# Two linked edits in an fp32 encoder trunk: block products accumulated over several blocks in the same PSUM banks, and the mixer's normalized input made on VectorE

## The chip, the cores and the metric

The kernel runs on one core of a Trainium2 chip. The metric is device time in microseconds of one execution. The kernel before takes 2313.22 us, the median of three runs that lie between 2312.47 and 2314.23.

In a profile, PE is TensorE, PEld its loading of weights, DVE VectorE, ACT ScalarE, POOL GpSimd, and SP the engine whose queue issues the transfers from and to memory.

## The reference

The program is a trunk of two layers over 512 positions and 1,024 features, in float32. Each layer is a half-step feed-forward network (FFN), a mixer, a second FFN and a gated embedding:

```python
for i in range(DEPTH):                                     # DEPTH = 2
    h = h + 0.5 * swiglu(rmsnorm(h, ffn1_norm[i]), ffn1_w_gu[i], ffn1_w_down[i])
    hn = rmsnorm(h, mix_norm[i])
    h = h + (ssd_mixer(hn, ...) if i % 2 == 0 else neighbourhood_attention(hn, ...))
    h = h + 0.5 * swiglu(rmsnorm(h, ffn2_norm[i]), ffn2_w_gu[i], ffn2_w_down[i])
    gate = jax.nn.sigmoid(rmsnorm(h, ple_norm[i]) @ ple_w_gate[i])
    h = h + gate * rmsnorm(p[i] @ ple_w_proj[i], ple_post_norm[i])

def swiglu(x, w_gu, w_down):                               # w_gu [1024, 5632], w_down [2816, 1024]
    g, u = jnp.split(x @ w_gu, 2, axis=-1)
    return (jax.nn.silu(g) * u) @ w_down
```

The mixer of layer 0 is a bidirectional state-space scan (SSD), which begins with a projection of `hn` to 8,256 columns; that of layer 1 is a neighbourhood attention.

## The kernel before

**Layout.** Features lie on the 128 partitions, positions on the free axis. h is 8 tiles of 128 x 512, and a weight is used in tiles of 128 x 128. TensorE accumulates in PSUM, in banks of 128 x 512 float32. Eight banks are in use: five of the kind `mm` and three of the kind `px`.

**Products in two halves.** Each operand is split into a high half, which is the value rounded to the fp32r type, and a low half, the rest. A product is then three: weight-high by x-high, weight-high by x-low, weight-low by x-high. `gemm` (lines 278, 281, 282) issues these three for 512 columns. The halves of a weight come from `split_raw`: a cast on ACT (L221) and a subtraction on DVE (L223). They are made by `prep_next` up to three units ahead of their use. Loads are issued on SP's queue (`load_unit`, `top_up`), and the order of units, which sets the order of loads too, is written out by `plan`. x is split by `split` (L303 to L307).

**FFN.** An FFN has 22 tiles of its inner width. The first few (`gate_up`, six in the first FFN, four in the others) are plain products. The others go in pairs of tiles, and each pair is computed by a scheme of seven products of half size in place of eight: x is cut into two halves of features and two halves of 256 positions, `sums` makes sums and differences of these (one set for each of kk = 0 to 3), `prep_next` makes sums and differences of the four weight matrices (L243, L246, L254), and `block(p, i)` with i = 0 to 6 multiplies the two. One block is 24 products of 256 columns: 2 output tiles, 4 tiles of features, and the three products of L508, L509 and L510. The four FFNs have 35 pairs, so 245 blocks. `block` takes a bank for each block and adds the results up from there (L514 on DVE, L518 on ACT), with `halve` splitting what goes into the second multiplication. Between blocks stand the products with the down weights, of 512 columns, eight per chunk of 14 or 21 blocks. `ffn_order` sets the sequence.

**SSD's start.** From h and the factor R of the norm (a row of 512, on all partitions) the normalized input is made: POOL multiplies by R (L687), and `split` then applies the gain in its cast on ACT (L306) and in its subtraction on DVE (L307). The steps of the scan's time constant (`steps`), the convolution (L748, L756) and the projection share the engines with this.

**What sets the order.** Each engine works through its own queue in order; a scheduler fixes the queues when the program is built, from the order in which the code is written and its estimate of durations, and puts in the waits. Buffers come from pools with a fixed number of slots; a new tile waits for the last reader of the slot's old one.

## Time and profile before

| | |
|---|---|
| time, median of 3 runs | 2313.22 us (2312.47 to 2314.23) |
| the profiled execution's own time | 2312.72 us |
| its span, first to last instruction | 2310.9 us |
| granted clock of TensorE, mean | 0.999 |
| DVE, POOL instructions | 2613, 269 |
| moved by DMA | 281.69 MB |

The page gives each engine's busy time and its share of the span, then the span in 40 slices, then the chain of work that ended last, then groups of instructions by line, operation and operands. A row of a group has the count, the busy time in us, the mean ns of one, and after the second bar the idle time of the engine just ahead of them with what ended it. A row of a timeline has the start, the duration, the engine, the line, the output and the inputs, the shape and the count; in square brackets it has the idle time before and what ended it. A row of waits has the us in total, how often, and the longest. A row of windows has the length and, by engine, the busy us with the count, then the granted clock, the share of the DMA engines and GB/s. Durations of neighbours on an engine can overlap, so the distance between two starts is the price of the first.

### The profile page before, as it was taken

Reading aid. Unit: us, or ns where it says so; the run is one execution under the profiler, and the core shown is the slowest. Engines: PE = TensorE matmul, PEld = TensorE weight load, DVE = VectorE, ACT = ScalarE, POOL = GpSimd, SP = SyncE. Lnnn points to the kernel's source line nnn. Section 1 sums busy time; section 2 is a strip of 40 time slices with the busy share of each in tenths; the row PEclk is TensorE's granted clock in tenths of the full one; section 3 lists DMA queues with packets and bytes.
Section 4 is the critical chain, followed back from the end, with each engine's and each line's share of the span. In section 5 each row is a group of like instructions: output and inputs, shape, how many; then the busy total and the mean of one; then the engine's idle time right before and its main releaser. Section 6 shows DMA issues by size and latency. Waiting matters only on the chain.

```text
span 2310.9 us, 35433 instructions
## 1 busy us (share of the span) xinstructions
PE 2294.1 (99%) x13732; PEld 2027.0 (88%) x13732; DVE 1828.3 (79%) x2613; ACT 1179.8 (51%) x2038; POOL 339.1 (15%) x269
## 2 busy tenths in 40 slices
PE   9999999999999999999999999999999999999999
PEld 8899997888888888999998889999878888999987
DVE  8878868878888958987875897887578859888866
ACT  5433445776767864443445443444446755444452
POOL 0000003255554651000003100000110010000020
PEclk9999999999999999999999999999999999999999
DMA  5323323444444643332223222232557732333222
GB/s 189 118 77 109 105 85 108 160 160 138 145 145 138 189 171 118 102 101 94 90 90 109 102 101 96 93 106 78 169 183 208 228 116 87 110 105 101 87 92 73
DMA packets 105224, 281.69 MB, mean 122 GB/s; under 512 B 13136, under 2 KB 14032, under 8 KB 105056
## 3 DMA queue, kind: packets, MB, share of 16 engines
q1 hardware_dynamic: 104768, 279.30, 37.3%
q8 instruction: 107, 1.75, 0.3%
q14 instruction: 61, 0.50, 0.1%
q10 hardware_dynamic: 288, 0.14, 0.0%
HBM read 259.70 MB, written 13.40 MB: 118 GB/s over the span
## 4 chain that ended last, share of the span: by engine, by line
PE 94%; DVE 3%; ACT 1%; DMA 1%; POOL 1%; issue 0%; SPq 0%; ACTq 0%
PE ps L278 19%; PE ps L281 19%; PE ps L282 19%; PE ps L510 10%; PE ps L509 10%; PE ps L508 10%; PE ps L930 1%; PE ps L889 1%; DVE wl L223 1%; PE ps L910 1%; PE ps L1325 1%; PE ps L1271 1%; DVE t L756 1%; PE ps L834 1%; POOL t L687 1%; PE ps L845 1%
## 5 line engine op out<-in xcount | busy, mean ns | idle before, releaser
L278 PE MATMUL ps<-md,wh 128*128 128x512 f32 (+1 forms) x2032 | 799.4, 394 | 2.6 <-ACT wh L221 1.8
L282 PE MATMUL ps<-md,wl 128*128 128x512 f32 (+1 forms) x2032 | 791.5, 390 | 2.8 <-DVE wl L223 2.8
L281 PE MATMUL ps<-md,wh 128*128 128x512 f32 (+1 forms) x2032 | 792.2, 390 | 0.0
L221 ACT CAST wh<-wr 128x1024 fp32r<-128x1024 f32 (+2 forms) x395 | 351.8, 892 | 491.7 <-PE ps L281 249.8
L223 DVE TENSOR_TENSOR wl<-wr,wh 128x1024 fp32r<-128x1024 f32 (+2 forms) x395 | 418.9, 1062 | 86.4 <-ACT wh L221 84.5
L282 PEld LDWEIGHTS ps<-md,wl 128*128 128x128 f32 x2032 | 382.1, 188 | 85.3 <-DVE wl L223 4.9
L278 PEld LDWEIGHTS ps<-md,wh 128*128 128x128 f32 x2032 | 382.8, 188 | 76.6 <-ACT wh L221 2.3
L281 PEld LDWEIGHTS ps<-md,wh 128*128 128x128 f32 x2032 | 382.8, 188 | 71.6
L221 ACT CAST wh<-md 128x1024 fp32r<-128x1024 f32 x175 | 183.6, 1049 | 322.6 <-PE ps L509 293.7
L332 POOL TENSOR_TENSOR sq<-sq,sq 128x512 f32<-128x512 f32 x71 | 101.0, 1423 | 1636.9 <-ACT sq L328 1632.5
L510 PE MATMUL ps<-sc,wl 128*128 128x256 f32 x980 | 277.6, 283 | 0.8 <-DVE wl L223 0.8
L508 PE MATMUL ps<-sc,wh 128*128 128x256 f32 x980 | 277.0, 283 | 0.8 <-ACT wh L221 0.8
L509 PE MATMUL ps<-md,wh 128*128 128x256 f32 x980 | 277.6, 283 | 0.1
L510 PE MATMUL ps<-md,wl 128*128 128x256 f32 x980 | 277.4, 283 | 0.0
L509 PE MATMUL ps<-sc,wh 128*128 128x256 f32 x980 | 277.3, 283 | 0.0
L508 PE MATMUL ps<-md,wh 128*128 128x256 f32 x980 | 277.2, 283 | 0.0
L514 DVE TENSOR_TENSOR t<-ps,t 128x512 f32<-128x512 f32 x245 | 165.9, 689 | 137.3 <-PE ps L510 136.6
L223 DVE TENSOR_TENSOR wl<-md,wh 128x1024 fp32r<-128x1024 f32 x175 | 213.6, 1220 | 16.1 <-ACT wh L221 15.7
L508 PEld LDWEIGHTS ps<-sc,wh 128*128 128x128 f32 x980 | 187.7, 192 | 4.9 <-ACT wh L221 1.0
L509 PEld LDWEIGHTS ps<-sc,wh 128*128 128x128 f32 x980 | 187.8, 192 | 3.8
L509 PEld LDWEIGHTS ps<-md,wh 128*128 128x128 f32 x980 | 188.1, 192 | 1.6 <-DVE md L472 0.4
L508 PEld LDWEIGHTS ps<-md,wh 128*128 128x128 f32 x980 | 188.1, 192 | 1.3
(209 smaller groups left out, 2913.2 us busy)
## 6 DMA issues: line engine op xcount, KB each, us to landing
wr<-in_w_gw_dram SPq DMA_DIRECT2D x70, 512.0 KB, 3.6
md<-in_w_gw_dram SPq DMA_DIRECT2D x70, 512.0 KB, 5.1
wr<-in_w_in_dram SPq DMA_DIRECT2D x65, 512.0 KB, 3.5
wr<-in_w_dn_dram SPq DMA_DIRECT2D x128, 256.0 KB, 2.7
wr<-in_w_gu_dram SPq DMA_DIRECT2D x32, 512.0 KB, 3.5
hs<-crow SPq DMA_DIRECT2D x64, 256.0 KB, 3.6
wr<-in_w_dn_dram SPq DMA_DIRECT2D x32, 384.0 KB, 3.1
wr<-in_w_qkv_dram SPq DMA_DIRECT2D x24, 512.0 KB, 4.3
```

The source lines that it names most:

```text
L221: splits.append(s.copy(out=hi[:, :n], in_=raw[:, :n]))
L223: v.tensor_sub(out=lo[:, :n], in0=raw[:, :n], in1=hi[:, :n])
L278: m = te.matmul(out=pt, lhsT=hi[:, sl], rhs=part(xp, 0, cols), start=first and k == 0, stop=False)
L281: te.matmul(out=pt, lhsT=hi[:, sl], rhs=part(xp, 1, cols), start=False, stop=False)
L282: gemm.last = te.matmul(out=pt, lhsT=lo[:, sl], rhs=part(xp, 0, cols), start=False, stop=last and k == n - 1)
L332: (v if fast else g).tensor_add(out=self.acc, in0=self.acc, in1=q)
L508: te.matmul(out=o, lhsT=hi[:, sl], rhs=xh, start=j == 0 and kk == 0, stop=False)
L509: te.matmul(out=o, lhsT=hi[:, sl], rhs=xl, start=False, stop=False)
L510: te.matmul(out=o, lhsT=lo[:, sl], rhs=xh, start=False, stop=j == 1 and kk == 3)
L514: v.tensor_add(out=k[to], in0=pt, in1=k[other])
L687: g.tensor_mul(out=t, in0=hk[k], in1=R)
L756: v.scalar_tensor_tensor(out=a[:, lo:hi], in0=src[:, lo + o:hi + o], scalar=w(j), in1=a[:, lo:hi], op0=ALU.mult, op1=ALU.add)
```

## The change

Blocks 0, 1, 2 and 6 no longer have a bank each. They accumulate in the same two banks (one for each output tile), one after the other, each starting from what the last one left. x's high and low half for them lie side by side in one tile of 512, so weight-high multiplies both as one product of 512 columns, and weight-low the high half as one of 256: 16 products per block instead of 24. A bank then holds the product with x's low half in its upper 256 columns and the rest in its lower 256; `whole` reads both parts and adds them, by a copy on ACT and an addition on DVE for each half. Blocks 3 and 5 accumulate in one bank in the old form, and block 4 has one. The order of blocks becomes 0, 3, 1, 5, 2, 4, 6, and the preparation of the next pair's weights stands at the same positions of the sequence as before. `sums` casts and subtracts in half pieces of 256. At SSD's start, POOL's multiplication and the gain are one operation on DVE, followed by a plain cast on ACT and a plain subtraction on DVE. The first product `cbm` of the first group takes a bank of the other kind.

```diff
--- before.py
+++ after.py
@@ -47,6 +47,9 @@
+TURN = (0, 3, 1, 5, 2, 4, 6)
 def ffn_order(chunks):
@@ -55,7 +58,7 @@
         a, b = chunks[c]
-        blocks = [(p, i) for p in range(a // 2, b // 2) for i in range(7)]
+        blocks = [(p, i) for p in range(a // 2, b // 2) for i in TURN]
         d = 0
...
@@ -166,8 +169,8 @@
                         yield "o", a
-                        if a[1] >= 4 and a[0] < NF // 2 - 1:
-                            yield from ahead(a[0] + 1, a[1] - 4)
+                        if a[1] in TURN[4:] and a[0] < NF // 2 - 1:
+                            yield from ahead(a[0] + 1, TURN.index(a[1]) - 4)
                     elif what == "down":
...
@@ -449,7 +452,7 @@
         xs = [[None] * 4 for _ in range(7)]
-        x11 = []
+        spare = []
...
@@ -461,15 +464,12 @@
                                        op1=ALU.mult)
-            if kk == 0:
-                x11[:] = [sc_r(), sc_r()]
-            elif kk == 2:
+            if kk == 2:
                 m = md(F32R)
-                x11[:] = m[:, 0, :], m[:, 1, :]
-            c = slice(HT * (kk % 2), HT * (kk % 2) + HT)
-            hl = x11[0][:, c], x11[1][:, c]
-            s.copy(out=hl[0], in_=x[0][:, lo_])
-            v.tensor_sub(out=hl[1], in0=x[0][:, lo_], in1=hl[0])
+                spare[:] = m[:, 0, :], m[:, 1, :]
+            hl = spare.pop(0) if spare else sc_r()
+            s.copy(out=hl[:, lo_], in_=x[0][:, lo_])
+            v.tensor_sub(out=hl[:, hi_], in0=x[0][:, lo_], in1=hl[:, lo_])
             xs[0][kk] = hl
...
@@ -481,68 +481,77 @@
                 return m[:, 0, :], m[:, 1, :]
-            (ah, al), (bh, bl) = room(), room()
             a, b = t2(), t2()
...
             v.tensor_sub(out=b[:, hi_], in0=x[1][:, lo_], in1=a[:, hi_])
-            for x_, hh, ll in ((a, ah, al), (b, bh, bl)):
-                s.copy(out=hh, in_=x_)
-                v.tensor_sub(out=ll, in0=x_, in1=hh)
-            for i, hh, ll, c in ((3, ah, al, lo_), (1, ah, al, hi_), (2, bh, bl, lo_), (6, bh, bl, hi_)):
-                xs[i][kk] = hh[:, c], ll[:, c]
+            for x_, two in ((a, (3, 1)), (b, (2, 6))):
+                for i, c, hl in zip(two, (lo_, hi_), room()):
+                    s.copy(out=hl[:, lo_], in_=x_[:, c])
+                    v.tensor_sub(out=hl[:, hi_], in0=x_[:, c], in1=hl[:, lo_])
+                    xs[i][kk] = (hl[:, lo_], hl[:, hi_]) if i == 3 else hl
...
-            pt = mm_bank()
+            k = kept
             hi, lo = unit()
+            chain = {0: "a", 1: "a", 2: "a", 6: "a", 3: "b", 5: "b", 4: "c"}[i]
+            opens, wide_ = i in (0, 3, 4), chain == "a"
+            if opens:
+                k[chain] = [mm_bank() for _ in range(1 + wide_)]
+            pt = k[chain]
+            mm = lambda o, w, x, st, sp_: te.matmul(out=o, lhsT=w, rhs=x, start=opens and st, stop=sp_,
+                                                    skip_group_check=not opens)
             for j in range(2):
...
                     sl = slice((4 * j + kk) * P, (4 * j + kk + 1) * P)
-                    o = pt[:, j * HT:(j + 1) * HT]
-                    xh, xl = xs[i][kk]
-                    te.matmul(out=o, lhsT=hi[:, sl], rhs=xh, start=j == 0 and kk == 0, stop=False)
-                    te.matmul(out=o, lhsT=hi[:, sl], rhs=xl, start=False, stop=False)
-                    te.matmul(out=o, lhsT=lo[:, sl], rhs=xh, start=False, stop=j == 1 and kk == 3)
-            k = kept
-            def add(to, other):
-                v.tensor_add(out=k[to], in0=pt, in1=k[other])
-            if i == 0:
-                k["s"] = t2()
-                s.copy(out=k["s"], in_=pt)
-            elif i == 1:
-                k["u"] = t2()
-                add("u", "s")
+                    last = kk == 3 and (wide_ or j == 1)
+                    if wide_:
+                        both = xs[i][kk]
+                        mm(pt[j], hi[:, sl], both, kk == 0, False)
+                        mm(pt[j][:, :HT], lo[:, sl], both[:, :HT], False, last)
+                    else:
+                        o = pt[0][:, j * HT:(j + 1) * HT]
+                        xh, xl = xs[i][kk]
+                        mm(o, hi[:, sl], xh, j == 0 and kk == 0, False)
+                        mm(o, hi[:, sl], xl, False, False)
+                        mm(o, lo[:, sl], xh, False, last)
+            def whole(to, more=False):
+                for j in range(2):
+                    o = to[:, j * HT:(j + 1) * HT]
+                    if more:
+                        v.tensor_add(out=o, in0=pt[j][:, HT:], in1=o)
+                    else:
+                        s.copy(out=o, in_=pt[j][:, HT:])
+                    v.tensor_add(out=o, in0=pt[j][:, :HT], in1=o)
+            if i in (0, 1):
+                to = "su"[i]
+                k[to] = t2()
+                whole(k[to])
+            elif i == 3:
+                k["q"] = t2()
+                s.copy(out=k["q"], in_=pt[0])
+            elif i in (5, 4):
+                to = "u" if i == 5 else "s"
+                v.tensor_add(out=k[to], in0=pt[0], in1=k[to])
+                s.activation(out=k[to], in_=k[to], func=AF.Silu)
             elif i == 2:
-                k["v"] = t2()
-                add("v", "u")
-            elif i == 3:
-                k["w"] = t2()
-                add("w", "v")
-                add("u", "u")
-            elif i == 4:
-                add("s", "s")
-                s.activation(out=k["s"], in_=k["s"], func=AF.Silu)
+                whole(k["q"], True)
+                v.tensor_mul(out=k["q"], in0=k["q"], in1=k["u"])
+                k["hl"] = md(F32R), md(F32R)
+                for j in range(2):
+                    mids[2 * p + j] = tuple(y[:, j, :] for y in k["hl"])
+                halve(k["hl"], k["q"], slice(HT, T))
             else:
-                if i == 5:
-                    add("u", "u")
-                    s.activation(out=k["u"], in_=k["u"], func=AF.Silu)
-                    x, gate, c = k["w"], k["u"], slice(HT, T)
-                    k["hl"] = md(F32R), md(F32R)
-                    for j in range(2):
-                        mids[2 * p + j] = tuple(y[:, j, :] for y in k["hl"])
-                else:
-                    add("v", "v")
-                    x, gate, c = k["v"], k["s"], slice(0, HT)
-                v.tensor_mul(out=x, in0=x, in1=gate)
-                halve(k["hl"], x, c)
+                w = t2()
+                whole(w)
+                v.tensor_mul(out=k["s"], in0=w, in1=k["s"])
+                halve(k["hl"], k["s"], slice(0, HT))
...
@@ -684,9 +693,9 @@
             t = t2()
-            g.tensor_mul(out=t, in0=hk[k], in1=R)
+            v.scalar_tensor_tensor(out=t, in0=hk[k], scalar=col(norm.gain + k), in1=R, op0=ALU.mult, op1=ALU.mult)
             xn.append(md(F32R))
-            split(xn[k], t, col(norm.gain + k))
+            split(xn[k], t, None)
...
@@ -840,7 +849,7 @@
             for dr in range(2):
-                pt = (mm_bank, px_bank)[dr]()
+                pt = (mm_bank if gi and dr == 0 else px_bank)()
                 for c in range(NC):
...
```

Line numbers shift: L223 becomes L226, L254 L257, L278, L281 and L282 become L281, L284 and L285, the products of a block are all L506, the split of the combinations of x (L492 and L493) is L491 and L492, the drains are L527, L529 and L530.

**The first place: TensorE, where the blocks of the third FFN begin.** Before, from the end of the first block (`wl_13108` is its weight's low half) into the second (`wl_13157`):

```order
L508 MATMUL ps_13193<-md_13084,wh_13106 128x256
L509 MATMUL ps_13193<-md_13084,wh_13106 128x256
L510 MATMUL ps_13193<-md_13084,wl_13108 128x256
L510 MATMUL ps_13230<-sc_12933,wl_13157 128x256
L508 MATMUL ps_13230<-sc_12995,wh_13155 128x256
L509 MATMUL ps_13230<-sc_12996,wh_13155 128x256
L510 MATMUL ps_13230<-sc_12995,wl_13157 128x256
L508 MATMUL ps_13230<-sc_13090,wh_13155 128x256
```

Now, from the end of block 0 (`wl_12744`) into block 3 (`wl_12797`):

```order
L506 MATMUL ps_12842<-md_12716,wh_12742 128x512
L506 MATMUL ps_12842<-md_12716,wl_12744 128x256
L506 MATMUL ps_12843<-md_12716,wl_12744 128x256
L506 MATMUL ps_12843<-md_12716,wh_12742 128x512
L506 MATMUL ps_12843<-md_12716,wl_12744 128x256
L506 MATMUL ps_12870<-sc_12562,wh_12795 128x256 x2
L281 MATMUL ps_12897<-md_12543,wh_12832 128x512
L284 MATMUL ps_12897<-md_12543,wh_12832 128x512
L506 MATMUL ps_12870<-sc_12562,wl_12797 128x256
L506 MATMUL ps_12870<-sc_12629,wh_12795 128x256 x2
L506 MATMUL ps_12870<-sc_12629,wl_12797 128x256
```

Block 0 alternates between products of 512 columns, with x's two halves in one operand, and of 256, and fills two banks. Two down products (L281, L284) have moved ahead of the next block's first product with its low half.

**The second place: VectorE at the same stretch.** L490 and L493 make combinations of x and their low halves, `wl_13157` is the weight's low half as above, L440 is the next plain product's. Before:

```order
L304 TENSOR_TENSOR md_13140<-t_13136,md_13140 128x512
L489 TENSOR_TENSOR t_13145<-t_13136,t_13145 128x256
L223 TENSOR_TENSOR wl_13157<-md_12871,wh_13155 128x1024
L490 TENSOR_TENSOR t_13146<-t_13136,t_13145 128x256
L493 TENSOR_TENSOR md_13143<-t_13145,md_13143 128x512
L254 TENSOR_TENSOR md_12871<-md_12789,md_12871 128x1024
L493 TENSOR_TENSOR md_13144<-t_13146,md_13144 128x512
L440 TENSOR_TENSOR t_13184<-ps_13104,rt_12899 128x512
L443 TENSOR_TENSOR t_13187<-ps_13105,rt_12899 128x512
```

Now, with `wl_12797` the weight's low half that TensorE's second block reads:

```order
L307 TENSOR_TENSOR md_12776<-t_12772,md_12776 128x512
L487 TENSOR_TENSOR t_12779<-t_12772,t_12779 128x256
L492 TENSOR_TENSOR md_12785<-t_12779,md_12785 128x256
L488 TENSOR_TENSOR t_12780<-t_12772,t_12779 128x256
L492 TENSOR_TENSOR md_12790<-t_12780,md_12790 128x256
L492 TENSOR_TENSOR md_12785<-t_12779,md_12785 128x256
L492 TENSOR_TENSOR md_12790<-t_12780,md_12790 128x256
L226 TENSOR_TENSOR wl_12797<-md_12493,wh_12795 128x1024
L443 TENSOR_TENSOR t_12823<-ps_12740,rt_12523 128x512
```

Four half pieces (L492) and L488 stand ahead of the weight's low half. Before, L490 and both L493 stood behind it, and so did L254, which is further back now.

**The third place: VectorE at SSD's start.** L681 scales the time constant, L748 the first product of the convolution, and `wl_3725` is the low half of the projection's weight that follows, and L756 is the convolution. Before, from the sixth of eight residuals (L307):

```order
L307 SCALAR_TENSOR_TENSOR md_3693<-t_3691,cst,md_3693 128x512
L307 SCALAR_TENSOR_TENSOR md_3698<-t_3696,cst,md_3698 128x512
L307 SCALAR_TENSOR_TENSOR md_3703<-t_3701,cst,md_3703 128x512
L748 TENSOR_TENSOR t_3711<-ps_3621,rt_3648 128x512
L223 TENSOR_TENSOR wl_3725<-wr_3569,wh_3723 128x1024
L756 SCALAR_TENSOR_TENSOR t_3713<-t_3711,ccw,t_3713 128x510
L223 TENSOR_TENSOR wl_3767<-wr_3575,wh_3765 128x1024
```

Now the same stretch's end, from the fifth of eight multiplications (L696) to the weight's low half `wl_3549`:

```order
L696 SCALAR_TENSOR_TENSOR t_3510<-hs_82,cst,rt_3472 128x512
L696 SCALAR_TENSOR_TENSOR t_3515<-hs_83,cst,rt_3472 128x512
L696 SCALAR_TENSOR_TENSOR t_3520<-hs_84,cst,rt_3472 128x512
L307 TENSOR_TENSOR md_3512<-t_3510,md_3512 128x512
L696 SCALAR_TENSOR_TENSOR t_3525<-hs_85,cst,rt_3472 128x512
L307 TENSOR_TENSOR md_3517<-t_3515,md_3517 128x512
L307 TENSOR_TENSOR md_3522<-t_3520,md_3522 128x512
L307 TENSOR_TENSOR md_3527<-t_3525,md_3527 128x512
L757 TENSOR_TENSOR t_3535<-ps_3445,rt_3472 128x512
L226 TENSOR_TENSOR wl_3549<-wr_3393,wh_3547 128x1024
```

Ahead of these stand L690 (which was L681), four L696 and four L307. DVE has 16 pieces where it had eight; POOL's queue is eight rows shorter.

## The prediction, made before the changed kernel ran

> **What bounds the kernel now.** I read the page first: shares, slices, the chain that ended last, the groups.
>
> ```profile
> span 2310.9 us, 35433 instructions
> PE 2294.1 (99%) x13732; PEld 2027.0 (88%) x13732; DVE 1828.3 (79%) x2613; ACT 1179.8 (51%) x2038; POOL 339.1 (15%) x269
> PEclk9999999999999999999999999999999999999999
> PE 94%; DVE 3%; ACT 1%; DMA 1%; POOL 1%; issue 0%; SPq 0%; ACTq 0%
> ...
> L510 PE MATMUL ps<-sc,wl 128*128 128x256 f32 x980 | 277.6, 283 | 0.8 <-DVE wl L223 0.8
> L514 DVE TENSOR_TENSOR t<-ps,t 128x512 f32<-128x512 f32 x245 | 165.9, 689 | 137.3 <-PE ps L510 136.6
> ```
>
> PE is busy for 99% of the span at full granted clock in all 40 slices, and the chain runs 94% through it. So the time is the sum of PE's steps, plus the few places where PE waits. Two things can move it: what a product costs PE, and whether PE waits more or less. The six 256-column groups (L508 to L510, 980 each) are the 5,880 products of 245 blocks. Their 283 ns of busy time overlaps the next product, so I take pace from starts on PE's timeline, in the SSD's projection and in the second FFN.
>
> ```profile
> 388.28 0.39 PE L281 MATMUL ps<-md,wh 128*128 128x512 f32 x1
> ...
> 401.88 0.39 PE L281 MATMUL ps<-md,wh 128*128 128x512 f32 x1
> ...
> 1001.58 0.39 PE L282 MATMUL ps<-md,wl 128*128 128x512 f32 x1
> 1001.81 0.28 PE L508 MATMUL ps<-sc,wh 128*128 128x256 f32 x1
> 1001.92 0.28 PE L509 MATMUL ps<-sc,wh 128*128 128x256 f32 x1
> ...
> 1004.56 0.28 PE L510 MATMUL ps<-md,wl 128*128 128x256 f32 x1
> 1004.68 0.40 PE L278 MATMUL ps<-md,wh 128*128 128x512 f32 x1
> 1004.91 0.40 PE L281 MATMUL ps<-md,wh 128*128 128x512 f32 x1
> 1005.15 0.39 PE L282 MATMUL ps<-md,wl 128*128 128x512 f32 x1
> ```
>
> The first two rows are 60 starts apart: 13.60/60 = 0.2267 us for 512 columns. From 1001.92 to 1004.56 lie 22 starts: 0.120 us for 256. Two narrow products cost 0.240, one wide 0.2267; the 13.3 ns between them is a cost per product, whatever its width.
>
> **Part 1, wide products.** Blocks 0, 1, 2 and 6 of each of 35 pairs (140 blocks) form eight groups of one 512- and one 256-column product instead of three of 256: 140 × 8 = 1,120 products fewer. Each group goes from 0.360 to 0.2267 + 0.120 = 0.3467 us, so the gain is 1,120 × 13.3 ns = **14.9 us**. What no row shows is the strict alternation of widths. The nearest rows are the switches above: 0.11 to 0.12 for a narrow product, 0.23 for a wide one beside it, 0.34 to 0.35 together (gain 11 to 22 us). The 0.24 at 1004.91 bounds it from the other side: with it the group costs 0.36 and the gain is nothing. I take the even paces, which lie inside the switches' range.
>
> The page "TensorE: Matmul & The Clock Gate" of the Trainium skill (section "Wait — 56ns, not 53.3ns?") puts the fixed cost of a warm matmul at about 2.5 ns; by it this term would be an estimated 2.8 us and the time 2308. The rows above show 13.3 ns between two narrow and one wide product, and the rows decide.
>
> **Part 2, chains and their drains.** Banks now accumulate over several blocks, and the next block of a chain can't start before the last value is read. Per pair DVE's seven full adds become two full and ten half ones, and ACT gets six half copies more. Rows that price them, from DVE's timeline at the second FFN's start, the groups by shape and the page's DMA issues:
>
> ```profile
> 944.83 0.68 DVE L304 TENSOR_TENSOR md<-t,md 128x512 fp32r<-128x512 f32 x1
> 945.43 0.42 DVE L489 TENSOR_TENSOR t<-t,t 128x256 f32<-128x256 f32 x1
> 945.77 1.22 DVE L223 TENSOR_TENSOR wl<-md,wh 128x1024 fp32r<-128x1024 f32 x1
> 946.90 0.42 DVE L490 TENSOR_TENSOR t<-t,t 128x256 f32<-128x256 f32 x1
> ...
> L698 ACT COPY sc<-ps 128x256 f32<-128x256 f32 x1 | 0.4, 353 | 0.0
> ...
> wr<-in_w_gw_dram SPq DMA_DIRECT2D x70, 512.0 KB, 3.6
> ```
>
> Steps (start to start) are 0.34 for a half piece, 0.60 for a full one and 1.13 for 1,024 columns. DVE gets 10 × 0.34 + 2 × 0.60 − 7 × 0.60 = 0.4 us more per pair, ACT 6 × 0.35 = 2.1. Over a steady stretch of blocks, and where the second FFN begins:
>
> ```profile
> core 0: us, PE busy (x) PEld busy (x) DVE busy (x) ACT busy (x) POOL busy (x), PEclk, DMA share, GB/s
> 915.00:955.00 40.00, 40.00 (x207) 34.30 (x206) 40.00 (x68) 24.11 (x36) 0.00 (x0) 1.00 0.27 87
> 990.00:1247.00 257.00, 257.00 (x1730) 238.32 (x1729) 198.23 (x248) 114.60 (x152) 13.84 (x10) 1.00 0.30 96
> ```
>
> In blocks DVE is busy for 198 of 257 us and ACT for 115; with the additions about 81% and 52%, so they fit beside PE. The order 0, 3, 1, 5, 2, 4, 6 puts another block (2.88 us, 24 × 0.12) and mostly a down product between two links. At the tightest place, the last chunk, where block 3 alone lies between 0 and 1, block 1 may start 8 × 0.3467 + 2.88 = 5.65 us after block 0 began. DVE's work queued there (0.60, 1.13, 0.60, 1.13 and two adds of 0.34, and 0.08 for the last one's tail) is done at 4.2. That leaves 1.4 us; a steady pair, walked in the same way, leaves 1.9. I cost the hand-overs at **0**; the cover is block 3, and without it each would cost up to those 2.9 us less the slack.
>
> On SP's queue one weight load moves ahead of a down load, and block 2's matrix is held two positions longer, so the load that takes its place starts later. It lands after 3.6 us; DVE has four pieces of 1.13 (4.5 us) to do before it reads that matrix. So again 0, with about 1 us of room; without it the loss would be under 1 us per pair and lie with the rival of slow hand-overs.
>
> **Part 3, FFN starts.** Here x's combinations are made while the first blocks begin, and DVE has no gap: 40.00 of 40.00 above. Each of four sets now takes four half subtractions instead of two full ones (+0.14 each). Worse, DVE's order puts four half pieces ahead of the low half of the second block's weight, where L490 and one of the full pieces came after it. The third FFN shows what that meets.
>
> ```profile
> PE ps L508 <- ACT wh L221: 0.8, 1, 0.8
> PE ps L510 <- DVE wl L223: 0.8, 1, 0.8
> ...
> 1354.64 1.21 DVE L223 TENSOR_TENSOR wl<-md,wh 128x1024 fp32r<-128x1024 f32 x1
> 1355.78 0.41 DVE L490 TENSOR_TENSOR t<-t,t 128x256 f32<-128x256 f32 x1
> ...
> 945.15 0.28 PE L508 MATMUL ps<-sc,wh 128*128 128x256 f32 x1
> ```
>
> The low half comes 0.34 (L490) + 4 × 0.34 + 3 × 0.14 = 2.1 us later. In the third FFN PE waits for it already, so all of **2.1** is lost. In the second, block 0 began at 945.15, the low half was wanted 26 products later (948.27) and was there at 946.90. Now it is there at 949.0 and wanted at 948.6 (block 0 is shorter by 0.11, two wide down products go ahead of it): 0.4 lost, and some 0.6 with the next low half: **1.0**. The fourth has the second's order, **1.0**; the first has room, **0.2**. Sum **+4.3 us**, ends 0 (the pieces fit) and 13 (each start trips the slow clock below and loses 1.6 to 2 us more).
>
> **Part 4, SSD's start.** POOL's eight multiplications go to DVE. Waits of PE between 340 and 450 us, and the timelines and clock around them:
>
> ```profile
> PE ps L282 <- DVE wl L223: 2.3, 2, 1.5
> PE ps L278 <- ACT wh L221: 1.8, 1, 1.8
> PE ps L716 <- DVE md L712: 1.4, 1, 1.4
> PE ps L278 <- DVE sc L848: 0.8, 1, 0.8
> ...
> 382.48 0.50 PE L278 MATMUL ps<-md,wh 128*128 128x512 f32 x1 [1.83 <-ACT wh L221]
> 384.06 0.50 PE L282 MATMUL ps<-md,wl 128*128 128x512 f32 x1 [0.85 <-DVE wl L223]
> ...
> 384.60:388.00 3.40, 3.40 (x9) 0.50 0.65 220
> ...
> 367.96 0.68 DVE L681 TENSOR_TENSOR t<-ps,rt 64x512 f32<-64x512 f32 x1 [1.87 <-ACT rt L359]
> 368.01 12.73 POOL L687 TENSOR_TENSOR t<-hs,rt 128x512 f32<-128x512 f32 x8 [10.75 <-ACT rt L359]
> 381.52 0.75 DVE L307 SCALAR_TENSOR_TENSOR md<-t,cst,md 128x512 fp32r<-128x512 f32 x1 [0.24 <-ACT md L306]
> 381.40 1.98 ACT L221 CAST wh<-wr 128x1024 fp32r<-128x1024 f32 x2
> ```
>
> POOL needs 12.7 us; ACT's casts and DVE's subtractions follow it one by one, and the weight's cast stands behind the last, at 381.40. Now DVE does 0.60 (L681) + 8 × 0.66 (the 0.75 of 381.52 less the 0.08 by which its rows overlap) + 8 × 0.60 from 367.96, is through at 378.6, and after L748's successor (0.60) and the subtraction (1.22) the low half is there at 380.5. PE wanted it at 382.48 − 1.83 + 2 × 0.2267 = 381.1. So the 1.83 and the 0.85 go, and with them the stretch at half clock behind (the window of 3.40 us with 9 products at 0.50: eight steps of 0.2267 take 1.8, so 1.6 us). The 1.46 of L282 (2.3 − 0.85) shrinks to about 0.5, the 1.4 of L716 (its DVE chain starts earlier) to about 0.3, and L848's 0.8 goes, since the first group takes another bank, with 0.5 left for that bank. 7.9 us of loss, 1.4 left: **−6.5**; ends +2 (DVE's longer run delays the dt chain) and −8.
>
> In these rows 1.83 + 0.85 us of waits close together were followed by 3.4 us at 0.50, L282's 1.46 by none. The same page ("Why this matters for your kernels") has the clock drop after some 3 us of idle array; by it none of the FFN waits would do that. By the row, the 2.9 us of the third FFN may: 1.6 us more, which lie in the first rival.
>
> **The sum** is made on the profiled execution, 2312.72 us (1.8 beside its span, 0.5 under the median of 2313.22): 2312.7 − 14.9 + 4.3 − 6.5 = 2295.6, on the median's scale **2296**.
>
> **Rivals.** (D) FFN starts lose more: 13 us instead of 4.3, **2305**. For it speaks a DVE without a gap there; against it the slack of 1.3 us in the second. (E) The SSD gain stays out: DVE is no earlier than POOL was. 10.1 us against 12.7 speaks against it. **2303**. (C) Alternating widths cost as much as three narrow products; the 0.24 step speaks for it, 0.23 + 0.12 against. **2310.5**. (B) The slower side: hand-overs stall PE. Each pair has three in the wide chain, 105 in all; a drain is two ACT copies and two DVE adds in line behind whole weight pieces, on a DVE at 81%. At 0.3 us each, 2296 + 31.5 = **2327**. It decides from 17.1/105 = 0.16 us per hand-over. DVE's 59 idle us in the 257 speak against it.
>
> **Numbers.** Forecast 0.62, D 0.14, E 0.08, C 0.06, B 0.08, others 0.02. The forecast's own range is 2289 to 2302; with D, E and half of C, 2287 to 2309. A difference under 0.2% (4.6 us) can't be told from none. Faster: the forecast, E, most of D, 0.83; same: half of C, the rest of D, some of B's milder cases, 0.08; slower: B and little else, 0.09.
>
> **What would show it.** Right: 1,120 products fewer on PE, wide block products 0.34 to 0.35 us per group on its timeline, no waits on drains at a chained block's first product, no half clock near 385 us, waits on low halves at the third FFN's start near 2.9 us. Wrong: groups at 0.36 (C), a wait of PE on drains in each pair (B), the weight's cast still at 381 (E), several clock drops at FFN starts (D).

## The result, and the profile after

The changed kernel takes **2306.63 us** (median of ten runs, 2305.39 to 2309.06) against 2313.60 us of the kernel before on the same chip (ten runs). The ratio is **0.9972, with an interval of 0.9963 to 0.9981**: 7.0 us faster, where 17.1 were forecast. The profiled execution took 2309.06 us, 3.66 less than the profiled one before. The page of the changed kernel begins:

```profile
span 2307.1 us, 33662 instructions
PE 2290.5 (99%) x12612; PEld 1967.2 (85%) x12612; DVE 1846.8 (80%) x2828; ACT 1246.9 (54%) x2280; POOL 324.2 (14%) x261
```

PE has the 1,120 products fewer (13,732 to 12,612), but its busy time fell by 3.6 us only. DVE's rose by 18 us and ACT's by 67, where the drains alone were worked out at 14 and 73.

To see where the time went, one instruction per stage serves as a milestone: the product that spreads a norm's factor over the partitions (L356, now L359). Its starts on PE's timeline in both profiled executions:

| ahead of | before | after | difference | gained or lost in the stage between |
|---|---|---|---|---|
| first FFN | 32.12 | 32.63 | +0.51 | +0.51, the program's start |
| SSD | 366.15 | 368.32 | +2.17 | +1.66, first FFN |
| second FFN | 914.30 | 908.92 | -5.38 | -7.55, SSD |
| embedding of layer 0 | 1246.54 | 1241.20 | -5.34 | +0.04, second FFN |
| third FFN | 1321.48 | 1316.14 | -5.34 | 0.00 |
| attention | 1670.59 | 1666.78 | -3.81 | +1.53, third FFN |
| fourth FFN | 1915.11 | 1911.28 | -3.83 | -0.02 |
| embedding of layer 1 | 2247.37 | 2243.54 | -3.83 | 0.00, fourth FFN |

All of the gain is the SSD's. The four FFNs, where the wide products are, gained nothing and lost 3.2 us. Two readings show why. The first is the pace. A chained block of the second FFN, from PE's timeline of the changed kernel:

```profile
1003.49 0.39 PE L506 MATMUL ps<-sc,wh 128*128 128x512 f32 x1
1003.72 0.28 PE L506 MATMUL ps<-sc,wl 128*128 128x256 f32 x1
1003.83 0.40 PE L506 MATMUL ps<-sc,wh 128*128 128x512 f32 x1
1004.06 0.28 PE L506 MATMUL ps<-sc,wl 128*128 128x256 f32 x1
1004.18 0.40 PE L506 MATMUL ps<-md,wh 128*128 128x512 f32 x1
1004.42 0.28 PE L506 MATMUL ps<-md,wl 128*128 128x256 f32 x1
...
1006.30 0.40 PE L506 MATMUL ps<-sc,wh 128*128 128x256 f32 x2
```

The eight groups take 2.81 us, 0.351 each, not 0.3467. In the steady stretch from 990 to 1225 us a wide product behind a narrow one takes 0.236 us on average, where 0.2267 is even, and the narrow one behind it 0.117. Over a whole pair of tiles the gain is smaller still. Between the same down product of two neighbouring pairs, before and after:

```profile
1035.80 0.40 PE L278 MATMUL ps<-md,wh 128*128 128x512 f32 x1
...
1066.92 0.40 PE L278 MATMUL ps<-md,wh 128*128 128x512 f32 x1
```
```profile
1031.60 0.40 PE L281 MATMUL ps<-md,wh 128*128 128x512 f32 x1
...
1062.49 0.40 PE L281 MATMUL ps<-md,wh 128*128 128x512 f32 x1
```

31.12 us became 30.89: 0.23 per pair, 7.2 ns for each of its 32 groups, 8.05 us for 35 pairs.

The second reading is the FFN starts. PE's waits over the whole span of the changed kernel (total, times, longest), and its waits and slow steps on the timeline where the second FFN's blocks begin:

```profile
PE ps L506 <- DVE wl L226: 4.3, 6, 2.6
PE ps L285 <- DVE wl L226: 2.9, 2, 2.3
...
PE ps L506 <- ACT wh L224: 0.6, 3, 0.2
```
```profile
943.07 0.39 PE L284 MATMUL ps<-md,wh 128*128 128x512 f32 x1
943.71 0.39 PE L506 MATMUL ps<-sc,wl 128*128 128x256 f32 x1 [0.25 <-DVE wl L226]
943.93 0.40 PE L506 MATMUL ps<-sc,wh 128*128 128x256 f32 x2
...
951.90 0.51 PE L506 MATMUL ps<-md,wh 128*128 128x256 f32 x2 [0.20 <-ACT wh L224]
952.42 0.50 PE L281 MATMUL ps<-md,wh 128*128 128x512 f32 x1
952.76 0.40 PE L284 MATMUL ps<-md,wh 128*128 128x512 f32 x1
953.55 0.39 PE L506 MATMUL ps<-md,wl 128*128 128x256 f32 x1 [0.40 <-DVE wl L226]
```

The first wait is the low half that the prediction spoke of, the second and third are block 5's weight. They add up to 0.85 us. But 943.07 to 943.71 is 0.64 for a step of 0.2267, so 0.41 for a wait of 0.25, and the product behind a wait takes 0.22 where 0.12 is even; 952.42 takes 0.34. The first of these surcharges comes from the way the profile counts: its wait begins at the end of the product ahead, 0.39 us after that one's start, while the next product would have begun 0.2267 after it. Adding up every step of PE that is over its even pace by more than 0.06 us, the four FFNs lost 4.3, 2.3, 6.6 and 2.2 us in the changed kernel, 0.9, 0.2, 3.0 and 0.1 before. The difference is **11.3 us**. Two stretches at half clock are in it, at the first and third FFN; the one of before, in the SSD, is gone (rows of windows, with PE alone):

```profile
57.00:60.40 3.40, 3.40 (x9) 0.51 0.87 284
384.60:388.00 3.40, 3.40 (x17) 1.00 0.69 236
1354.00:1357.40 3.40, 3.40 (x15) 0.50 0.61 225
```

They cost about 1.6 us each. So in the profiled execution: -8.05 (pace) + 11.3 (FFN starts) - 7.6 (SSD) + 0.5 (start) = -3.8 against -3.66 measured. Without the two stretches it would be -7.0. That this equals the difference of the medians is partly chance, since the profiled execution before was 0.9 us under its median. But the ten runs do differ in this way: their mean granted clock is 1.000 in the two fastest and 0.998 in the two slowest.

### The profile page after: what moved, and what is told of

Read it like the earlier page. It is cut to its first block, busy times and chain, and to the rows that moved or that the text cites. A ratio compares the mean times of both kernels' runs of the same rounds, so it can differ in the third digit from the quotient of the medians.

```text
span 2307.1 us, 33662 instructions
## 1 busy us (share of the span) xinstructions
PE 2290.5 (99%) x12612; PEld 1967.2 (85%) x12612; DVE 1846.8 (80%) x2828; ACT 1246.9 (54%) x2280; POOL 324.2 (14%) x261
## 4 chain that ended last, share of the span: by engine, by line
PE 77%; DVE 10%; issue 6%; ACT 4%; DMA 1%; POOL 1%; SPq 0%; POOLq 0%; ACTq 0%; DVEq 0%
PE ps L506 30%; PE ps L281 14%; PE ps L285 14%; PE ps L284 14%; DVE wl L226 2%; DVE t L765 2%; ACT sc L812 1%; ACT sc L809 1%; ACT wh L224 1%; DVE sc L951 1%; DVE md L307 1%; PE ps L1280 1%; PE ps L1334 1%; ACT t L761 1%; ACT t L768 1%
## 5 line engine op out<-in xcount | busy, mean ns | idle before, releaser
L281 PE MATMUL ps<-md,wh 128*128 128x512 f32 (+1 forms) x2032 | 800.4, 394 | 0.0
L285 PE MATMUL ps<-md,wl 128*128 128x512 f32 (+1 forms) x2032 | 792.2, 390 | 2.9 <-DVE wl L226 2.9
L284 PE MATMUL ps<-md,wh 128*128 128x512 f32 (+1 forms) x2032 | 790.9, 389 | 0.0
L226 DVE TENSOR_TENSOR wl<-wr,wh 128x1024 fp32r<-128x1024 f32 (+2 forms) x395 | 418.5, 1061 | 110.3 <-ACT wh L224 108.3
L285 PEld LDWEIGHTS ps<-md,wl 128*128 128x128 f32 x2032 | 382.2, 188 | 86.2 <-DVE wl L226 4.3
L281 PEld LDWEIGHTS ps<-md,wh 128*128 128x128 f32 x2032 | 382.2, 188 | 75.3 <-ACT wh L224 1.0
L284 PEld LDWEIGHTS ps<-md,wh 128*128 128x128 f32 x2032 | 382.5, 188 | 72.6 <-DVE md L559 0.2
L506 PE MATMUL ps<-md,wh 128*128 128x256 f32 (+1 forms) x1610 | 367.1, 308 | 0.6 <-ACT wh L224 0.6
L506 PE MATMUL ps<-sc,wh 128*128 128x512 f32 (+1 forms) x1190 | 362.9, 357 | 0.1
L506 PE MATMUL ps<-sc,wl 128*128 128x256 f32 x980 | 276.5, 282 | 3.1 <-DVE wl L226 3.1
L506 PEld LDWEIGHTS ps<-md,wh 128*128 128x128 f32 x1610 | 261.2, 189 | 21.4 <-ACT wh L224 1.5
L506 PE MATMUL ps<-md,wl 128*128 128x256 f32 x980 | 277.0, 283 | 1.2 <-DVE wl L226 1.2
L226 DVE TENSOR_TENSOR wl<-md,wh 128x1024 fp32r<-128x1024 f32 x175 | 214.0, 1223 | 64.9 <-ACT wh L224 60.4
L506 PEld LDWEIGHTS ps<-sc,wh 128*128 128x128 f32 x1190 | 210.3, 189 | 34.7 <-ACT wh L224 0.5
L506 PEld LDWEIGHTS ps<-sc,wl 128*128 128x128 f32 x980 | 185.2, 189 | 9.1 <-DVE wl L226 4.4
L506 PEld LDWEIGHTS ps<-md,wl 128*128 128x128 f32 x980 | 185.4, 189 | 3.8 <-DVE wl L226 3.7
L580 DVE SCALAR_TENSOR_TENSOR hs<-ps,hs 128x512 f32<-128x512 f32 x160 | 110.0, 687 | 82.3 <-PE ps L285 82.0
L765 DVE SCALAR_TENSOR_TENSOR t<-ps,ccw,t 128x510 f32<-128x510 f32 (+1 forms) x180 | 133.9, 744 | 10.7 <-ACT t L761 8.0
L530 DVE TENSOR_TENSOR t<-ps,t 128x256 f32<-128x256 f32 x280 | 115.9, 418 | 7.1 <-ACT t L529 4.7
```

The lines of the kernel that those rows point to most:

```text
L226: v.tensor_sub(out=lo[:, :n], in0=raw[:, :n], in1=hi[:, :n])
L281: m = te.matmul(out=pt, lhsT=hi[:, sl], rhs=part(xp, 0, cols), start=first and k == 0, stop=False)
L284: te.matmul(out=pt, lhsT=hi[:, sl], rhs=part(xp, 1, cols), start=False, stop=False)
L285: gemm.last = te.matmul(out=pt, lhsT=lo[:, sl], rhs=part(xp, 0, cols), start=False, stop=last and k == n - 1)
L506: mm = lambda o, w, x, st, sp_: te.matmul(out=o, lhsT=w, rhs=x, start=opens and st, stop=sp_, skip_group_check=not opens)
L530: v.tensor_add(out=o, in0=pt[j][:, :HT], in1=o)
```

## The experiments

Each kernel ran beside the kernel before. A difference between two other kernels is one of medians, and the intervals of the ratios are 2 to 3.6 us to either side, so about 1 us between two of them is not shown by the times alone.

**What each part is worth.** Three kernels have one part of the change each. The first is the kernel before with only the edits in the SSD:

```diff
-            g.tensor_mul(out=t, in0=hk[k], in1=R)
+            v.scalar_tensor_tensor(out=t, in0=hk[k], scalar=col(norm.gain + k), in1=R, op0=ALU.mult, op1=ALU.mult)
             xn.append(md(F32R))
-            split(xn[k], t, col(norm.gain + k))
+            split(xn[k], t, None)
...
-                pt = (mm_bank, px_bank)[dr]()
+                pt = (mm_bank if gi and dr == 0 else px_bank)()
```

> The kernel before with only the edits outside the FFNs: the residual of the SSD's input on VectorE, and the first group's product in a bank of the other kind. Theory from the two profiles: the stage's gain of 7.9 us less 0.3 at its end stands by itself, so 2306 us (2305 to 2307), with PE's waits of 1.83, 0.85 and 1.40 us and the half clock behind them gone. Rival: the gain needs the FFN edits too (another order of weights when the stage begins); then 2309 to 2313.

Measured 2305.88 us, ratio 0.9968 (0.9955 to 0.9980). The small part of the change alone is as fast as all of it. With only the first of its two edits:

> The kernel before with the SSD's residual on VectorE and nothing else: the first group's product keeps its old bank. Theory: nearly all of the stage's gain is the residual's, and the bank is worth the 0.8 us that PE waited for it: 2306.7 us (2306 to 2307.5), 0.8 above the kernel with both. Rival: the bank's wait was in the shadow of the residual's delay and goes with it: 2305.9.

Measured 2307.21 us, 0.9973 (0.9963 to 0.9984). PE then waits 1.4 us for the bank (0.8 before), so the bank is worth about 1.3 us and the residual 6.3 (the two intervals overlap, the runs do not). The other way round, the changed kernel with the two edits undone:

> The changed kernel with the SSD's residual back on POOL and the first group's bank as before. Theory: the block edits gain 9.3 us by wide products and lose about as much at the four FFN starts, so with the SSD's 7.6 us given back this is 2314 us (2312 to 2317), not faster than before. Rival, by the prediction's terms (14.9 gained, 4.3 lost): 2303.

Measured 2316.59 us, 1.0015 (1.0006 to 1.0024). The block edits alone make the kernel slower, by 3.3 us. The parts don't add up to the whole (-7.4 and +3.3, together -4.1, against -7.0). This kernel's runs have a mean clock of 0.997 to 0.999, those of the changed kernel 0.998 to 1.000, which would be a stretch at half clock or two; that these are all of the 2.9 us was not shown.

**The pace.** In the changed kernel each wide product is issued as two narrow ones:

```diff
-                        mm(pt[j], hi[:, sl], both, kk == 0, False)
+                        mm(pt[j][:, :HT], hi[:, sl], both[:, :HT], kk == 0, False)
+                        mm(pt[j][:, HT:], hi[:, sl], both[:, HT:], False, False)
```

> The changed kernel with each product of 512 columns of a block issued as two of 256, into the two halves of the same bank; chains, drains, sums and order stay. Theory: a group of three narrow products costs 0.360 us and the wide one with its narrow neighbour 0.352, as the trace of the changed kernel has it, so 1,120 x 8.3 ns = 9.3 us more than the changed kernel: 2316 us (2314 to 2319). Rival, the prediction's paces (0.360 and 0.3467): 14.9 us more, 2321.5. Second rival, alternating widths gain nothing: 2306.6, as the changed kernel.

Measured 2314.67 us (2312.79 to 2316.54), ratio to before 1.0005 (0.9996 to 1.0014). Against the changed kernel this is 8.0 us, the 8.05 of the pairs' period; 14.9 is excluded. In its trace the same down product of two neighbouring pairs is 31.12 us apart again, as in the kernel before:

```profile
1032.30 0.40 PE L281 MATMUL ps<-md,wh 128*128 128x512 f32 x1
...
1063.42 0.40 PE L281 MATMUL ps<-md,wh 128*128 128x512 f32 x1
```

So the steady gain is that of the wide products; the chains and the new order of blocks neither add to it nor take from it. If switching the width is the reason why it is small, products sorted by width must be faster (the lines added):

```diff
+                    for kk in range(4):
+                        mm(pt[j], hi[:, sls[kk]], xs[i][kk], kk == 0, False)
+                    for kk in range(4):
+                        mm(pt[j][:, :HT], lo[:, sls[kk]], xs[i][kk][:, :HT], False, kk == 3)
```

> The changed kernel with the order of products in a chained block changed: for each bank the four of 512 columns first, then the four of 256, instead of in turn. Theory: the 5 ns by which a wide and a narrow product together miss the sum of their even paces are the price of a switch of width; with one switch to and fro per four pairs it is 3/4 x 5 ns x 1,120 = 4.2 us faster than the changed kernel, 2302.4 us. Rival: after a switch the wide pace stays above 0.2267 us for several products (the down products behind a block start at 0.233, 0.24, 0.23, 0.23), so four in a row pay as much: 2306 to 2308.

Measured 2303.10 us, 0.9952 (0.9938 to 0.9965): 3.5 us faster than the changed kernel with the same products, and no run of the one overlaps with one of the other. PE's timeline of this kernel, one chained block:

```profile
1001.63 0.61 PE L506 MATMUL ps<-sc,wh 128*128 128x512 f32 x2
1002.08 0.62 PE L506 MATMUL ps<-md,wh 128*128 128x512 f32 x2
1002.53 0.40 PE L506 MATMUL ps<-sc,wl 128*128 128x256 f32 x2
1002.77 0.40 PE L506 MATMUL ps<-md,wl 128*128 128x256 f32 x2
1003.01 0.63 PE L506 MATMUL ps<-sc,wh 128*128 128x512 f32 x2
1003.48 0.62 PE L506 MATMUL ps<-md,wh 128*128 128x512 f32 x2
1003.94 0.40 PE L506 MATMUL ps<-sc,wl 128*128 128x256 f32 x2
1004.17 0.40 PE L506 MATMUL ps<-md,wl 128*128 128x256 f32 x2
1004.41 0.40 PE L506 MATMUL ps<-sc,wh 128*128 128x256 f32 x2
```

Four wide products take 0.90 and 0.93 us, four narrow ones 0.48 and 0.47, and the block 2.78 in place of 2.81, or 0.3475 per group: nearly the even paces. 140 blocks by 0.03 us are 4.2, and a whole pair takes 30.74 us (L281 at 1029.61 and at 1060.35) in place of 30.89, about 5 us for 35 pairs. So most of what alternation lost was the price of the switches. The 3.5 us measured are less than the trace has; two kernels at the end of this section that differ in this alone, without half clock in their profiles, are 4.6 us apart.

**The FFN starts.** First the one edit that the prediction held against them, alone in the kernel before:

```diff
-                s.copy(out=hh, in_=x_)
-                v.tensor_sub(out=ll, in0=x_, in1=hh)
+                for c in (lo_, hi_):
+                    s.copy(out=hh[:, c], in_=x_[:, c])
+                    v.tensor_sub(out=ll[:, c], in0=x_[:, c], in1=hh[:, c])
```

> The kernel before with x's combinations cast and subtracted in half pieces of 256, as the change does, and nothing else; nothing is left out. It takes from the change the one edit that the prediction held against the FFN starts. Theory: the half pieces alone put three of them ahead of the third FFN's low half (1.1 us with the longer sets, and a clock drop in some runs), delay the first FFN's by about 1, and cost the other two nothing, since their low half had 1.3 us of room: 2315 us (2314.5 to 2317). Rival: the half pieces cost nothing and the waits come from the new order of blocks and its earlier sums: 2313.3.

Measured 2317.32 us, 1.0017 (1.0008 to 1.0026): 3.9 us, twice what I expected, and most of it in the first FFN. PE's waits from 30 to 80 us, in the kernel before, in this one and in the changed one:

```profile
PE ps L282 <- DVE wl L223: 0.5, 1, 0.5
```
```profile
PE ps L282 <- DVE wl L223: 1.9, 1, 1.9
```
```profile
PE ps L285 <- DVE wl L226: 2.3, 1, 2.3
```

The half pieces alone make most of that wait. So they are a cause; what else is, three moves in the changed kernel tell. In the first, the pieces for blocks 2 and 6 are made later (`later` is emptied behind a plain round, for the last two sets behind block 0):

```diff
-            for x_, two in ((a, (3, 1)), (b, (2, 6))):
+            halves_of(a, (3, 1))
+            later.append(lambda: halves_of(b, (2, 6)))
```

> The changed kernel with one thing moved: of each set of x's combinations, the halves for blocks 2 and 6 (a cast on ACT and a subtraction on VectorE each, four pieces per set) are made one plain round later, for the last two sets behind block 0. Nothing is left out. Theory: the FFN starts lose their time to the low halves of weights that stand behind those pieces on VectorE; they come 0.7 us or more earlier, most of the waits and with them the half clock go, 2299 to 2302 us. Rival: the waits come from late loads or from the banks that the chains hold: 2305 to 2309, as the changed kernel.

Measured 2305.48 us, 0.9965 (0.9951 to 0.9978): 1.1 us better than the changed kernel, which the times can't tell from nothing: the expectation failed. The mechanism held in the trace, though, and the wait moved on. At the third FFN the wait of 2.6 us is 1.27, followed by three of 0.3 to 0.5. In the second FFN the low half's 0.25 us is gone, and one remains (a block's products are L510 in this kernel):

```profile
952.75 0.50 PE L510 MATMUL ps<-sc,wh 128*128 128x512 f32 x1 [0.48 <-ACT wh L224]
```

The product is 512 columns wide, so it is one of block 2. Its weight's cast on ACT (951.63) stands behind the cast of block 5's weight (949.90), a down weight's (950.85) and a drain. The first FFN still waited 2.19 us: there the second set's other pieces stand ahead of the low half, and ACT's cast of that weight waited 1.3 us for its load. Block 5's weight and the first FFN have a move each:

```diff
-TURN = (0, 3, 1, 5, 2, 4, 6)
+TURN = (0, 3, 1, 4, 2, 5, 6)
```

(with the product of gate and value moved from block 2 to block 5, where both are there).

> The changed kernel with blocks in the order 0, 3, 1, 4, 2, 5, 6: block 5, whose weight is a sum that VectorE makes last, comes two places later; the three hand-overs of the wide chain still have a block between them. Theory: the waits at three FFN starts for block 5's weight (0.2 and 0.4 us, with the slow products that follow each, about 1.2 in all) are due to its early place: 3 x 1.2 = 3.6 us faster than the changed kernel, 2303 us. Rival: the next block's weight is as late, since VectorE's queue has no gap there; 2306 to 2307.

Measured 2301.61 us, 0.9949 (0.9937 to 0.9962): 5.0 us better, 1.4 more than expected. The slow steps of the second and fourth FFN fall from 2.3 and 2.2 to 0.8 and 0.7. Part of the rest lies at the first FFN of the profiled execution, where PE waits 1.7 us in place of 2.3 and no stretch at half clock follows; why was not tested.

```diff
-                if left and R[0] is not None:
+                if left and R[0] is not None and not first:
                     sums(left.pop(0))
+                more = R[0] is not None
                 gate_up(a[0])
+                if left and first and more:
+                    sums(left.pop(0))
```

> The changed kernel with one thing moved in the first FFN alone: the second and third set of x's combinations are made behind the plain products of their round instead of ahead of them. Theory: PE's wait of 2.3 us at 53 us, and the half clock behind it in some runs, come from the pieces of the second set that stand ahead of a weight's low half on VectorE: 1.7 to 3.3 us faster, 2303 to 2305. Rival: the weight's load lands late (ACT's cast waited 1 us for it), then 2306 to 2307.

Measured 2305.45 us, 0.9964 (0.9951 to 0.9976). By the median it is 1.2 us, less than expected. In its profile no wait is left between 30 and 80 us, and the slow steps of that FFN are 0.6 instead of 4.3; its fastest run, with a mean clock of 1.000, took 2303.44 against 2305.39. Its runs spread up to 2306.50, with mean clocks down to 0.998; the third FFN's wait of 2.6 us is untouched, here with the clock at 1.00 behind it.

> The changed kernel with three moves together: halves for blocks 2, 5 late as tried before (those of blocks 2 and 6), blocks in the order 0, 3, 1, 4, 2, 5, 6, and the first FFN's sets behind their plain products. Theory: each takes away its own waits, 1.1 + 3.6 + 2.5 us: 2299.5. Rival: VectorE's whole work ahead of the blocks sets the time there, whatever its order: 2303 to 2306.

Measured **2296.49 us**, 0.9927 (0.9915 to 0.9940): 10.1 us under the changed kernel. So it was the order of the work, and not its amount, that set the time there: VectorE's 2,828 instructions are the same, two of the moves shift some of them behind the piece that PE waits for, and the third shifts the block that needs a late weight. The slow steps of the four FFNs are 0.3, 0.3, 3.4 and 0.1, about those of the kernel before. With the products sorted by width as well, and then with one more piece late in the last set:

> The three moves tried together before (halves for blocks 2 and 6 late, blocks in the order 0, 3, 1, 4, 2, 5, 6, the first FFN's sets behind their plain products), and the products of a chained block by width, four wide and four narrow for each bank. Theory: the two gains lie at different places, so 2296.5 less 3.5 us: 2293. Rival: the block that is shorter meets later weights and the gain is lost to waits: 2296.

> The same with one more move: the last set's split for blocks 4 and 5 (0.60 us on VectorE) also behind block 0. Theory: the third FFN's wait for a low half (1.27 us with the moves above) shrinks by 0.6: 2292.4, 0.6 below the kernel with four moves. Rival: another weight is late behind it, and the time is the same.

Measured 2291.91 us, 0.9906 (0.9890 to 0.9921), and 2291.48 us, 0.9904 (0.9891 to 0.9918). The first is 1 us better than expected. The second can't be told from the first: PE's one wait for a low half at the third FFN is 1.2 us in it and 1.5 in the other, 0.3 less where 0.6 was expected. Both beat the kernel before by 21.5 to 22 us and the changed one by 15. The second's page and the wait:

```profile
PE 2278.2 (100%) x12612; PEld 1964.8 (86%) x12612; DVE 1842.5 (80%) x2828; ACT 1244.6 (54%) x2280; POOL 324.8 (14%) x261
...
PE ps L513 <- DVE wl L226: 1.2, 1, 1.2
```

## Why the prediction was right or wrong

| term | forecast | measured |
|---|---|---|
| wide products | -14.9 | -8.0 |
| hand-overs of the chains | 0 | 0 |
| FFN starts | +4.3 | +8.1, and 11.3 with the half clock |
| SSD's start | -6.5 | -7.6 |
| the program's start | none | +0.5 |
| sum | -17.1 | -7.0 |

**The direction** was right, and its size was wrong by more than half; the time lies in the range only because of the rivals that it took in. Of the 10.1 us between forecast and result, the wide products account for 6.9 and the FFN starts for 3.8; the SSD's start, 1.1 better than forecast, hides a little of it.

**Part 1 failed at one step**: "I take the even paces, which lie inside the switches' range". The rows for the price of a switch were quoted there (0.23 and 0.12, and 0.24 after a block), and the value taken, 14.9, was in the upper half of bounds from 0 to 22 us; 8.0 was measured. Those rows show one switch between long rows of equal widths. In strict alternation the wide product is slower, 0.236 us. The mechanism, a fixed cost per product, stands: sorted by width the paces are nearly the even ones. In alternation about 6 of the 13.3 ns are lost again, 7.2 are left. The rival with alternating widths, held at 6%, was half true: a group costs neither 0.3467 nor 0.36.

**Part 2 was right.** The wait list has no wait of PE for a drain, and in a steady stretch of blocks PE has no gap, with DVE at 79% (81% forecast, though the prediction's own 0.4 us per pair on 198 of 257 us gives 78%; the row has PE, PEld, DVE, ACT and POOL in this order):

```profile
990.00:1247.00 257.00, 257.00 (x1494) 226.58 (x1493) 202.18 (x286) 128.97 (x198) 15.12 (x11) 1.00 0.30 99
```

The slower rival, stalls at hand-overs, fell. The change could still have come out slower without the SSD's edits, by another mechanism: the block edits alone cost 3.3 us.

**Part 3 had the right mechanism and too small a price.** DVE's rows at the third FFN are as the order gave them:

```profile
1349.32 0.42 DVE L492 TENSOR_TENSOR md<-t,md 128x256 fp32r<-128x256 f32 x1
1349.66 0.42 DVE L488 TENSOR_TENSOR t<-t,t 128x256 f32<-128x256 f32 x1
1349.99 1.22 DVE L492 TENSOR_TENSOR md<-t,md 128x256 fp32r<-128x256 f32 x3
1351.13 1.22 DVE L226 TENSOR_TENSOR wl<-md,wh 128x1024 fp32r<-128x1024 f32 x1
```

The low half's subtraction begins at 1351.13. Before it began at 1354.64, which less this stage's offset of 5.34 is 1349.30: 1.8 us later (2.1 forecast). The five pieces between 1349.32 and 1351.13 are all of it; the 0.42 that the prediction added for longer sets does not show, and both full pieces, not one, had stood behind before. PE's wait there was 2.6 (2.9 forecast), and those of the second FFN 0.85 (1.0). Three things were missing. First, a wait costs about 0.26 us more than the profile's figure for it: the steps around the three short ones of the second FFN lost 1.9 us for 0.85 of waiting (a further short delay, at 952.13, is in it). Second, "the first has room, 0.2" was wrong: its low half already made PE wait 0.5 before, and the wait became 2.3. Third, the half clock: the prediction saw it behind waits of 2.7 us, left it out of its own sum and put it into a rival; in the profiled execution it came at two of the four starts, behind waits of 2.3 and 2.6. That rival (13 us at the FFN starts, 14%) was nearest to what happened: 8 to 11.

**Part 4 was right**, with 7.6 for 6.5: the half clock and the waits went, L285's wait for the low half is 0.63 (0.5 forecast), and the low half was there at 382.67, which less the stage's offset of 2.17 is the 380.5 that was worked out. L725's wait and the bank's, 0.3 and 0.5 in the sum, are not there. (The remainders add up to 1.3 us, not the 1.4 that the sum took.)

```profile
381.46 1.21 DVE L226 TENSOR_TENSOR wl<-wr,wh 128x1024 fp32r<-128x1024 f32 x1
...
PE ps L285 <- DVE wl L226: 0.6, 1, 0.6
```

## What to carry to other kernels

Take the price of a mix of operations from rows in which they are mixed; the sum of two even paces is its best case, and here sorting the products by size gave 3.5 to 4.6 us back. Where an engine has no gap at the start of a stage, count what an edit puts ahead of the one piece that PE waits for, not what it adds in total: moving work that is needed later behind it, and a block whose weight is late to a later place, gained 10 us with the same work. A wait removed shows the next one in line, so moves that are small one by one are tried together.

## What the runs showed of the hardware

A wide and a narrow product in turn take 0.351 us in a block, sorted by width 0.3475; the cost of a switch shows on the wide product (0.236 us on average behind a narrow one, where 0.2267 is even).

A wait of PE cost about 0.26 us more than the profile gives for it (0.25 waited, 0.41 + 0.10 lost; 2.60 waited at the third FFN, 2.76 + 0.10 lost): 0.16 is overlap with the product ahead that is lost, and the first product behind runs 0.1 us over its pace.

Waits of 1.9 us (`before_half`, first FFN), 2.3 and 2.6 us (the changed kernel) were followed, 1 to 2 us later, by 3.4 us at a granted clock of about 0.5; a wait of 1.9 us in `narrow`'s first FFN and one of 2.6 us in `first_after`'s third were not:

```profile
1349.50:1352.90 3.40, 3.40 (x23) 1.00 0.53 175
```

The Trainium skill ("TensorE: Matmul & The Clock Gate", "Part 1: The HAM clock gate") has the clock fall after an idle window of about 3.4 us that runs freely, and the count of slow products at a kernel's start differ from run to run because of it. The difference between runs agrees with that, though no run here shows the window itself; a wait shorter than the window was enough here, so the lesson for a sum is that a wait of about 2 us has a chance to cost 1.6 us more.
